# Hybrid decoder trunk: queries and keys as one product of 512 columns, pooling in alternating column halves, banks filled one by one, output weights prepared with a lead

## The chip, the cores and the metric

One core of a Trainium2 chip runs the whole program. The metric is the device time of one execution in microseconds. Three executions of the kernel before gave 939.35, 939.42 and 940.2 us; the median is 939.42. Profiles were taken of one execution each; there times are counted from the span's first instruction.

## The reference, cut to what matters

The trunk has two layers over 256 tokens of 1024 features. Each layer is a half-step feed-forward part, a mixer and another half-step feed-forward part, all in float32:

```
for l in range(DEPTH):                                  # DEPTH = 2
    x = x + 0.5 * swiglu(rms_norm(x, ffn1_norm[l]), ffn1_gate[l], ffn1_up[l], ffn1_down[l])
    h = rms_norm(x, mix_norm[l]) @ w_in[l]               # 1024 -> 18 blocks of 128
    y_pool = pool_mixer(u_pool, pool_w[l], pool_scale[l])
    y_moba = moba_attention(rope(qm), rope(km), vm)      # causal over 256 tokens, 4 heads of 64
    y_dil  = dilated_attention(rope(qd), rope(kd), vd)   # three dilations merged, 4 heads of 64
    y_conv = conv_module(u_conv, ...)                    # gate, 31 taps, layer norm, silu
    x = x + concatenate([y_pool, y_moba, y_dil, y_conv]) @ w_out[l]
    x = x + 0.5 * swiglu(rms_norm(x, ffn2_norm[l]), ffn2_gate[l], ffn2_up[l], ffn2_down[l])
return rms_norm(x, final_norm)
```

The inner width of the feed-forward parts is 2816, that is 22 blocks of 128. With 256 tokens, the whole attention of a head fits into 256 x 256 scores.

## The kernel before, in words

**Weights in two halves.** Every weight is used as a sum of two reduced-precision parts. Weights come in units of 128 x 2048 (a gate and an up block, half a down block, two blocks of the input projection or a quarter of the output projection). `prep` (L485) makes a unit ready in two halves: a load into one of four raw buffers (`RAW`), a ScalarE copy into the reduced type (`hi`), and a VectorE subtraction that gives the rest (`lo`). Five units can be ready at a time (`RING`, L41); a unit takes the place of the fifth one before it. The normed input is held the same way, `hi` and `lo` side by side. A product is then three terms, `hi` x `hi`, `hi` x `lo` and `lo` x `hi`.

**Gate, up and down.** `pair_unit` (L651) multiplies a gate and an up block with the input: 8 chunks of the contraction, two column blocks c with a PSUM bank each. `halves` (L624) issues for a list of (chunk, bank) items first all passes of one kind and then of the other: with `lo` weights a pass of 256 columns, with `hi` weights one of 512 (both parts of the input in one pass). The kind that comes first alternates from call to call. In `pair_units` (L639) the list runs over chunks, and inside over units and the two banks, so that the two banks take turns. The first unit behind a norm is issued in `BLOCKS` of chunks (0 to 3, 4 and 5, 6, 7), since the normed input comes chunk by chunk. At the start of the program three units are computed together, chunk by chunk, as their pieces arrive. Seven of the eight banks are given out by age (`oldest`).

**The mixer.** `mix` (L723) computes the convolution's gate and input with `pair_unit`, then, with tokens on the partitions, query and key of the dilated attention, values of both, query and key of the other attention, and the pooling input. `by_tokens` (L773) does one of them from one unit: 8 chunks x 2 token halves x 3 terms = 48 passes of 256 columns. `rope` (L786) calls it, copies the result out with a scale, rotates the first 16 features of each head by four small VectorE steps, transposes it back in four blocks and copies it out. The values (L840 to L853) are one product over two units with 512 columns per pass. `scores`, `softmax` and `pv` are the attention; `pv` issues its products for the two 64-column halves of the array in turn. Pooling (L885 to L907): after its input comes a product with a banded matrix for each of four groups (`psw`), a copy, a product with the group's weights (`psp`) and the copies out. The 31 taps of the convolution run on VectorE, the first four with help from ScalarE, then come bias, layer norm over the features (two rounds of small matmuls) and the last activation. The output projection (L943 to L952) takes four units in the order `W_OUT`: dilated attention, pooling, other attention, convolution; each is 48 passes of 256 columns.

**Order.** The program is first recorded as a list of operations with an estimated cost for each. `Plan.order` (L170) simulates the engines: each takes, of the operations that are ready, the one with the earliest due time, less a `lead` where one is set (L200 to L202); the order found is emitted, and on the chip every engine follows it strictly. `LEAD` (L51) is 0. The costs given to `mm`, `together` and `transpose` serve only this simulation.

**The end.** The last norm (L983 to L1015) needs its statistics, a transposed row of factors, and eight multiplications of 128 x 256 with stores: seven by VectorE out of PSUM, one by GpSimd from a copy that ScalarE made, whose store ScalarE issues. The program begins with ten warm-up matmuls (`WARM`, L46).

Of the kernel before, what the change touches and what calls it, by code (L numbers as in the profile page):

```python
# [16 lines left out]
T = 256  # L17
# [28 lines left out]
WARM = 10  # L46
# [4 lines left out]
LEAD = 0  # L51
# [19 lines left out]
class View:  # L71
# [23 lines left out]

    def heads(self):
        return self._then(lambda t: t.to_broadcast([128, 2, 4, t.shape[3]]))
# [166 lines left out]
def trunk(ctx: ExitStack, tc: tile.TileContext, d):  # L264
# [154 lines left out]
    units = []  # L419
    for l in range(DEPTH):  # L420
        for w in range(2):
# [63 lines left out]
    def prep():  # L485
# [5 lines left out]
        plan.lead = LEAD  # L491
# [76 lines left out]
    class Norm:  # L568
# [35 lines left out]
        def row(self, after):  # L604

            plan.hold = after
            for t in range(2):
                transpose(0.11, self.ps.on(t)[:, t * 128:(t + 1) * 128], self.col[:, t:t + 1].to_broadcast([128, 128]))
# [30 lines left out]
    def pair_units(nrm, names, blocks=ALL):  # L639
# [83 lines left out]
    def mix(l, nrm, after):  # L723
# [49 lines left out]
        def by_tokens(nm):  # L773
# [12 lines left out]
        def rope(i, j, nm, col):  # L786

            ps = by_tokens(nm)
            q = slot(i, f"{nm}t{l}")
            for t in range(2):  # L790
                A(T, q.on(t)[:, t], ps.on(t)[:, t], AF.Copy, scale=col[:, t:t + 1])
            v = q.rearrange("p t (h e) -> p t h e", h=4)
            a = work("ra", 2, [128, 2, 4, 16], f"ra_{nm}{l}")
            b = work("rb", 2, [128, 2, 4, 16], f"rb_{nm}{l}")
            tt(64, "tensor_mul", b.on(0)[:, :, :, 0:8], v[:, :, :, 8:16], sin_t[:, :, :, 0:8].heads())
            tt(64, "tensor_mul", b.on(1)[:, :, :, 8:16], v[:, :, :, 0:8], sin_t[:, :, :, 8:16].heads())
            tt(128, "tensor_mul", a, v[:, :, :, 0:16], cos_t.heads())
            tt(128, "tensor_add", v[:, :, :, 0:16], a, b)
            ps = bank("qk", 2, [128, 2, T], f"tr_{nm}{l}")
            for t in range(2):  # L800
                for c in range(2):
                    transpose(0.11, ps.on(2 * t + c)[:, c, t * 128:(t + 1) * 128], q[:, t, c * 128:(c + 1) * 128])
# [301 lines left out]
```

## Time and profile before

| what | us |
|---|---|
| median of three executions (939.35 to 940.2) | 939.42 |
| the profiled execution | 939.52 |
| its span, first to last instruction | 937.7 |
| TensorE matmul busy | 925.4 |
| VectorE busy | 717.7 |
| ScalarE busy | 561.7 |
| GpSimd busy | 33.6 |
| gate and up matmuls, share of the chain that ended last | 50% |
| down matmuls, share of that chain | 26% |

Busy time counts an engine as busy from the start to the end of an instruction. TensorE's matmuls overlap each other, so what one costs in a stream is read from the starts of two groups and not from its own duration. A stretch's wait is found in the idle time in brackets at the end of a timeline's row, with the engine that ended it. PE is TensorE, PEld its weight loads, DVE VectorE, ACT ScalarE.

### The profile page before, as it was taken

Reading aid. Unit: us, or ns where it says so; the run is one execution under the profiler, and the core shown is the slowest. Engines: PE = TensorE matmul, PEld = TensorE weight load, DVE = VectorE, ACT = ScalarE, POOL = GpSimd, SP = SyncE. Lnnn points to the kernel's source line nnn. Section 1 sums busy time; section 2 is a strip of 40 time slices with the busy share of each in tenths; the row PEclk is TensorE's granted clock in tenths of the full one; section 3 lists DMA queues with packets and bytes.
Section 4 is the critical chain, followed back from the end, with each engine's and each line's share of the span. In section 5 each row is a group of like instructions: output and inputs, shape, how many; then the busy total and the mean of one; then the engine's idle time right before and its main releaser. Section 6 shows DMA issues by size and latency. Waiting matters only on the chain.

```text
span 937.7 us, 15041 instructions
## 1 busy us (share of the span) xinstructions
PE 925.4 (99%) x5646; PEld 823.1 (88%) x5646; DVE 717.7 (77%) x1328; ACT 561.7 (60%) x1050; POOL 33.6 (4%) x46
## 2 busy tenths in 40 slices
PE   9999999999999999999999999999999999999996
PEld 8888888898898888888888888888988988888885
DVE  7789986679879988766778886668788989886652
ACT  7666664559576765554556565445667757555540
POOL 0000000100002000000100000011000200000010
PEclk9999999999999999999999999999999999999998
DMA  8855666762075765456755555567513476654641
GB/s 297 270 212 187 188 175 203 235 216 101 10 239 181 246 210 193 125 168 190 253 203 186 183 191 138 164 195 250 184 46 113 159 251 222 209 173 137 187 124 45
DMA packets 55209, 170.17 MB, mean 181 GB/s; under 512 B 6368, under 2 KB 8416, under 8 KB 55136
## 3 DMA queue, kind: packets, MB, share of 16 engines
q1 hardware_dynamic: 54560, 168.79, 55.7%
q8 instruction: 44, 0.72, 0.3%
q10 hardware_dynamic: 576, 0.42, 0.2%
q14 instruction: 29, 0.24, 0.1%
HBM read 168.14 MB, written 1.05 MB: 180 GB/s over the span
## 4 chain that ended last, share of the span: by engine, by line
PE 92%; DMA 3%; ACT 2%; DVE 2%; SPq 0%; issue 0%; ACTq 0%; DVEq 0%
PE mm_gu L368 50%; PE dn L368 26%; DMA raw<-in_gu_dram 3%; PE v L368 2%; PE wo L368 2%; PE pu L368 1%; PE qd L368 1%; PE qm L368 1%; PE kd L368 1%; PE km L368 1%; PE mm_cg L368 1%; PE mm_ca L368 1%; DVE y_f L346 1%; ACT hi L312 1%; DMA x<-in_x_dram 0%; DVE x L312 0%
## 5 line engine op out<-in xcount | busy, mean ns | idle before, releaser
L312 DVE TENSOR_TENSOR lo<-raw,hi 128x1024 fp32r<-128x1024 f32 (+3 forms) x365 | 386.3, 1085 | 68.1 <-ACT hi L312 54.4
L312 ACT ACTIVATE hi<-raw 128x1024 fp32r<-128x1024 f32 (+3 forms) x365 | 328.5, 940 | 136.1 <-PE dn L368 53.7
L368 PE MATMUL mm_gu<-y_f,hi 128*128 128x512 f32 x1408 | 332.4, 391 | 1.1 <-DVE t L312 0.8
L368 PEld LDWEIGHTS mm_gu<-y_f,hi 128*128 128x128 f32 x1408 | 260.6, 189 | 54.9 <-DVE y_f L346 1.9
L368 PEld LDWEIGHTS mm_gu<-y_f,lo 128*128 128x128 f32 x1408 | 176.1, 191 | 4.1
L368 PE MATMUL mm_gu<-y_f,lo 128*128 128x256 f32 x1408 | 178.3, 283 | 0.0
L368 PE MATMUL dn<-h,hi 128*128 128x512 f32 x704 | 169.4, 390 | 0.0
L368 PEld LDWEIGHTS dn<-h,hi 128*128 128x128 f32 x704 | 128.7, 188 | 24.1
L312 DVE TENSOR_TENSOR t<-mm_gu,t 128x256 f32<-128x256 f32 x176 | 66.9, 418 | 52.1 <-ACT t L312 51.7
L368 PEld LDWEIGHTS dn<-h,lo 128*128 128x128 f32 x704 | 91.5, 191 | 4.3
L368 PE MATMUL dn<-h,lo 128*128 128x256 f32 x704 | 92.8, 282 | 0.0
L312 ACT ACTIVATE h<-th 128x256 fp32r<-128x256 f32 x88 | 36.5, 417 | 70.2 <-DVE th L312 70.2
L312 ACT ACTIVATE t<-mm_gu 128x256 f32<-128x256 f32 x176 | 56.8, 375 | 26.9 <-PE mm_gu L368 26.8
L312 ACT ACTIVATE th<-t 128x256 f32<-128x256 f32 x88 | 36.7, 417 | 41.1 <-DVE t L312 31.1
L312 DVE TENSOR_TENSOR t<-t,rb_f 128x512 f32<-128x512 f32 x88 | 60.1, 686 | 0.8
L346 DVE SCALAR_TENSOR_TENSOR x<-dn,x 128x256 f32<-128x256 f32 x64 | 27.0, 422 | 38.0 <-PE dn L368 37.4
L368 PE MATMUL wo<-mx,hi 128*128 128x256 f32 x256 | 48.4, 289 | 0.0
L346 DVE SCALAR_TENSOR_TENSOR yv<-hpad,par,yv 128x256 f32<-128x256 f32 x108 | 44.3, 478 | 0.0
L312 DVE TENSOR_TENSOR th<-th,t 128x256 f32<-128x256 f32 x88 | 36.9, 420 | 9.0 <-ACT th L312 8.6
L368 PEld LDWEIGHTS wo<-mx,hi 128*128 128x128 f32 x256 | 39.9, 191 | 0.2
L312 DVE TENSOR_TENSOR h<-th,h 128x256 fp32r<-128x256 f32 x88 | 36.3, 418 | 1.1 <-ACT h L312 1.1
L368 PE MATMUL wo<-mx,lo 128*128 128x256 f32 x128 | 36.4, 284 | 0.0
(211 smaller groups left out, 677.0 us busy)
## 6 DMA issues: line engine op xcount, KB each, us to landing
raw<-in_gu_dram SPq DMA_DIRECT2D x170, 512.0 KB, 4.4
raw<-in_dn_dram SPq DMA_DIRECT2D x64, 384.0 KB, 3.6
raw<-in_dn_dram SPq DMA_DIRECT2D x64, 320.0 KB, 2.9
raw<-in_wi_dram SPq DMA_DIRECT2D x36, 512.0 KB, 4.4
raw<-in_wo_dram SPq DMA_DIRECT2D x16, 512.0 KB, 4.1
raw<-in_gu_dram SPq DMA_DIRECT2D x9, 256.0 KB, 5.7
con<-in_con_dram SPq DMA_DIRECT2D x1, 932.0 KB, 8.2
x<-in_x_dram SPq DMA_DIRECT2D x3, 256.0 KB, 5.7
```

The costliest lines, as they stand in the source:

```text
L312: f(*[val(x) for x in a], **{n: val(x) for n, x in k.items()})
L346: nc.vector.scalar_tensor_tensor(out, in0=a, scalar=scalar, in1=b, op0=op0, op1=op1)
L368: nc.tensor.matmul(val(o), lhsT=val(lhsT), rhs=val(rhs), start=self.i == 0, stop=self.i == self.n - 1, skip_group_check=True)
```

## The change

Queries and keys of one attention are computed by one product over two units, in the form that the values had (`wide`); `by_tokens` remains for the pooling input. `rope` then works by token half: two copies out, four rotation steps over the eight heads of query and key, four transposes; two copies at the end. The weights are laid out accordingly. In `pair_units` the banks are the outermost loop of a list. Pooling alternates between the two 64-column halves with each product, in two groups. Preparing an output unit (its loads, copies and subtractions) has a lead of 6 us in the planner. There is one warm-up matmul fewer; some of the planner's costs are changed; and at the end VectorE does all eight multiplications in order and SyncE issues all stores.

```diff
-WARM = 10
+WARM = 9
-LEAD = 0
+LEAD = 6.0
...
-    units = []
+    units, output = [], set()
...
                 for k in range(4):
+                    output.add(len(units))
                     units.append((d["wo"][l, k], 16))
...
-        plan.lead = LEAD
+        plan.lead = LEAD if n in output else 0.0
...
-            transpose(0.11, ps.on(t)[:, t * 128:(t + 1) * 128], y[:, t:t + 1].to_broadcast([128, 128]))
+            transpose(0.09, ps.on(t)[:, t * 128:(t + 1) * 128], y[:, t:t + 1].to_broadcast([128, 128]))
...
             i = halves([(s[u][c], ps[u][c], parts[u](2 * k + c), nrm.y[k])
-                        for k in range(a, b) for u in range(len(names)) for c in range(2)])
+                        for c in range(2) for k in range(a, b) for u in range(len(names))])
...
-                    s.mm(0.326, ps.on(t)[:, t], (xh, w[0]), (xh, w[1]), (xl, w[0]))
+                    s.mm(0.36, ps.on(t)[:, t], (xh, w[0]), (xh, w[1]), (xl, w[0]))
...
+        def wide(nm):
+
+            ps = [bank("mm", 4, [128, 512], f"{nm}{l}{t}") for t in range(2)]
+            sm = [Sum(), Sum()]
+            for u in range(2):
+                part = take()
+                for t in range(2):
+                    sl = slice(t * 128, (t + 1) * 128)
+                    for i in range(4):
+                        y = nrm.y[u * 4 + i]
+                        wh, wl = part(4 * i, 4)
+                        xh, xl = y.on(0)[:, 0, sl], y.on(1)[:, 1, sl]
+                        sm[t].mm(0.68, ps[t], (xh, wh), (xh, wl), (xl, wh))
+            return ps
+
+        def rope(i, j, nm):
+
+            ps = wide(f"qk{nm}")
+            out = [bank("qk", 2, [128, 2, T], f"tr_{n}{nm}{l}") for n in "qk"]
             for t in range(2):
+                qk = flat(slot(i + t, f"qk{nm}t{l}{t}"))
+                for n, col in enumerate((qcol, nrm.col)):
+                    s = slice(n * T, (n + 1) * T)
+                    A(T, qk.on(n)[:, s], ps[t][:, s], AF.Copy, scale=col[:, t:t + 1])
...
+                for n in range(2):
+                    for c in range(2):
+                        f = n * T + c * 128
+                        transpose(0.09, out[n].on(2 * t + c)[:, c, t * 128:(t + 1) * 128], qk[:, f:f + 128])
+            res = []
+            for n in range(2):
+                res.append(slot(j + n, f"{'qk'[n]}{nm}{l}"))
+                A(512, res[n], out[n], AF.Copy)
+            return res
...
-        qd = rope(8, 14, "qd", qcol)
-        kd = rope(9, 15, "kd", nrm.col)
+        qd, kd = rope(8, 14, "d")
...
-            together(1.8, *items)
+            together(1.45, *items)
...
-        qm = rope(8, 23, "qm", qcol)
-        km = rope(9, 24, "km", nrm.col)
+        qm, km = rope(8, 23, "m")
...
-        sw = [Sum(), Sum()]
-        for g in range(4):
-            c, e = g // 2, g % 2
-            o = psw.on(g)[64 * e:64 * e + 64, c]
-            ch = slice(64 * g, 64 * g + 64)
-            a = C_PW + g * PWN
-            sw[e].mm(0.14, o[:, 0:144], (ut.on(0)[:, 0, ch], con[:, a:a + 144]))
-            sw[e].mm(0.13, o[:, 128:256], (ut.on(1)[:, 1, ch], con[:, a + 144:a + 272]))
+        for c in range(2):
+            sw = [Sum(), Sum()]
+            o = [psw.on(c)[64 * e:64 * e + 64, c] for e in range(2)]
+            ch = [slice(64 * g, 64 * g + 64) for g in (2 * c, 2 * c + 1)]
+            a = [C_PW + g * PWN for g in (2 * c, 2 * c + 1)]
+            together(0.5, *[(sw[e], o[e][:, 0:144], ut.on(0)[:, 0, ch[e]], con[:, a[e]:a[e] + 144]) for e in range(2)],
+                     *[(sw[e], o[e][:, 128:256], ut.on(1)[:, 1, ch[e]], con[:, a[e] + 144:a[e] + 272])
+                       for e in range(2)])
...
-    row = work("sq", 2, [128, T], "row_fin")
-    A(T, row, ps[:, 0:T], AF.Copy)
-    for j in (6, 0, 1, 2, 3, 4, 5, 7):
+    for j in range(KC):
         o = scaled[j // 2].on(j % 2)[:, j % 2]
-        if j == 6:
-            gg(T, "tensor_mul", o, o, row)
-        else:
-            tt(T, "tensor_mul", o, o, ps[:, 0:T])
-        if j in (0, 1, 7):
+        tt(T, "tensor_mul", o, o, ps[:, 0:T])
+        if j in (0, 1, KC - 2, KC - 1):
             store(d["out"][:, j:j + 1], scaled[j // 2].on(j % 2)[:, j % 2:j % 2 + 1], 256)
-        elif j == 6:
-            rec("act", 0.47, nc.scalar.dma_start, [], [o], (), {
-                "out": d["out"][:, j:j + 1], "in_": scaled[j // 2].on(0)[:, 0:1]})
```

## Rows read from the trace of the kernel before

**Rows 1.** The page's first part: busy time, share of the span, instructions.
```profile
PE 925.4 (99%) x5646; PEld 823.1 (88%) x5646; DVE 717.7 (77%) x1328; ACT 561.7 (60%) x1050; POOL 33.6 (4%) x46
```

**Rows 2.** TensorE's waits, whole span: us in total, times, longest.
```profile
PE psp L368 <- ACT pl L312: 1.5, 2, 0.7
PE st_fin L312 <- DVE y_fin L346: 1.2, 1, 1.2
...
PE mm_gu L368 <- DVE t L312: 0.8, 1, 0.8
```

**Rows 3.** Windows: stretch, busy time (instructions) by engine, PEclk, DMA share, GB/s.
```profile
203.30:255.80 52.50, 51.76 (x393) 46.36 (x392) 45.23 (x137) 36.34 (x84) 0.00 (x0) 1.00 0.21 72
...
927.50:937.70 10.20, 1.39 (x11) 0.98 (x9) 3.97 (x14) 1.46 (x4) 0.72 (x1) 0.72 0.28 103
```

**Rows 4.** Timeline of TensorE, gate stage: start, us, instruction, tiles, shape, count.
```profile
28.03 4.00 PE L368 MATMUL mm_gu<-y_f,lo 128*128 128x256 f32 x32
31.86 7.44 PE L368 MATMUL mm_gu<-y_f,hi 128*128 128x512 f32 x32
39.14 4.00 PE L368 MATMUL mm_gu<-y_f,lo 128*128 128x256 f32 x32
```

**Rows 5.** Chain that ended last, first mixer: start, us on the chain, what.
```profile
218.96 2.06 PE v L368 x9
...
224.32 5.03 PE v L368 x21
229.34 5.75 PE qm L368 x48
...
237.62 0.44 PE tr_qm L312 x4
...
246.59 1.45 PE pv_d L380 x16
```

**Rows 6.** Timeline of TensorE, end of the first mixer's attention; idle before in brackets.
```profile
252.65 1.20 PE L368 MATMUL psw<-con,ut 128*64 128x144 f32 x16
254.59 1.13 PE L368 MATMUL psp<-pl,plw 128*128 128x256 f32 x4 [0.74 <-ACT pl L312]
...
255.99 0.39 PE L368 MATMUL wo<-mx,lo 128*128 128x256 f32 x1
...
263.62 0.70 PE L368 MATMUL ln<-yv,mean_w 128*128 128x256 f32 x2
```

**Rows 7.** Timeline of VectorE, same stretch and the seam behind it.
```profile
251.68 0.48 DVE L346 SCALAR_TENSOR_TENSOR yv<-hpad,par,yv 128x256 f32<-128x256 f32 x1
...
254.72 2.34 DVE L312 TENSOR_TENSOR lo<-raw,hi 128x1024 fp32r<-128x1024 f32 x2
...
275.15 0.75 DVE L346 SCALAR_TENSOR_TENSOR mx<-yv,mx 128x256 fp32r<-128x256 f32 x2
...
279.01 1.23 DVE L312 TENSOR_TENSOR lo<-raw,hi 128x1024 fp32r<-128x1024 f32 x1 [1.95 <-ACT hi L312]
```

**Rows 8.** Timeline of TensorE's weight loads at the start.
```profile
10.37 0.30 PEld L368 LDWEIGHTS mm_gu<-y_f,hi 128*128 128x128 f32 x2 [0.17 <-ACT hi L312]
...
11.59 0.30 PEld L368 LDWEIGHTS mm_gu<-y_f,hi 128*128 128x128 f32 x2 [0.34 <-ACT hi L312]
...
24.50 0.30 PEld L368 LDWEIGHTS mm_gu<-y_f,hi 128*128 128x128 f32 x2 [1.18 <-DVE t L312]
```

**Rows 9.** Timeline of TensorE, first unit of the second feed-forward part.
```profile
282.88 1.61 PE L368 MATMUL mm_gu<-y_f,hi 128*128 128x512 f32 x6
284.74 0.73 PE L368 MATMUL mm_gu<-y_f,hi 128*128 128x512 f32 x2 [0.25 <-DVE y_f L346]
```

**Rows 10.** Groups by shape, the warm-up: busy us, mean ns, idle before.
```profile
L368 PE MATMUL warm<-mean_w 128*128 128x128 f32 x20 | 4.6, 429 | 1.0 <-POOL half_pi L312 1.0
```

**Rows 11.** Timeline, all engines, the last norm.
```profile
931.33 0.38 ACT L312 ACTIVATE row_fin<-st_fin 128x256 f32<-128x256 f32 x1 [1.43 <-PE st_fin L312]
931.74 2.41 DVE L312 TENSOR_TENSOR xg<-xg,st_fin 128x256 f32<-128x256 f32 x7 [0.99 <-ACT row_fin L312]
```

More of the change, by code (lines that the diff above doesn't have):

```diff
@@ L782, in by_tokens @@
                     xh, xl = nrm.y[k].on(0)[:, 0, sl], nrm.y[k].on(1)[:, 1, sl]
-                    s.mm(0.326, ps.on(t)[:, t], (xh, w[0]), (xh, w[1]), (xl, w[0]))
+                    s.mm(0.36, ps.on(t)[:, t], (xh, w[0]), (xh, w[1]), (xl, w[0]))
             return ps
-        def rope(i, j, nm, col):
-            ps = by_tokens(nm)
-            q = slot(i, f"{nm}t{l}")
-            for t in range(2):
[L791 to L802, printed above, removed]
-            out = slot(j, f"{nm}{l}")
-            A(512, out, ps, AF.Copy)
-            return out
@@ new lines, in rope @@
+        def rope(i, j, nm):
+            ps = wide(f"qk{nm}")
+            out = [bank("qk", 2, [128, 2, T], f"tr_{n}{nm}{l}") for n in "qk"]
+            for t in range(2):
+                qk = flat(slot(i + t, f"qk{nm}t{l}{t}"))
+                for n, col in enumerate((qcol, nrm.col)):
+                    s = slice(n * T, (n + 1) * T)
+                    A(T, qk.on(n)[:, s], ps[t][:, s], AF.Copy, scale=col[:, t:t + 1])
+                v = qk.rearrange("p (h e) -> p h e", h=8)
+                a = work("ra", 2, [128, 8, 16], f"ra_{nm}{l}{t}")
+                b = work("rb", 2, [128, 8, 16], f"rb_{nm}{l}{t}")
+                sin, cos = sin_t[:, t], cos_t[:, t]
+                tt(64, "tensor_mul", b.on(0)[:, :, 0:8], v[:, :, 8:16], sin[:, :, 0:8].to_broadcast([128, 8, 8]))
+                tt(64, "tensor_mul", b.on(1)[:, :, 8:16], v[:, :, 0:8], sin[:, :, 8:16].to_broadcast([128, 8, 8]))
+                tt(128, "tensor_mul", a, v[:, :, 0:16], cos.to_broadcast([128, 8, 16]))
+                tt(128, "tensor_add", v[:, :, 0:16], a, b)
+                for n in range(2):
[7 more added lines that the diff above has]
+            return res
@@ L833, in softmax @@
             return p
-        qd = rope(8, 14, "qd", qcol)
-        kd = rope(9, 15, "kd", nrm.col)
+        qd, kd = rope(8, 14, "d")
         pd = [p for c in range(2) for p in scores(qd, kd, c, C_BD, f"d{l}", 16)]
-        psv = [bank("mm", 4, [128, 512], f"v{l}{t}") for t in range(2)]
+        psv = wide("v")
         vt = [flat(slot(20 + t, f"vt{l}{t}")) for t in range(2)]
-        sv = [Sum(), Sum()]
-        for u in range(2):
-            part = take()
-            for t in range(2):
-                sl = slice(t * 128, (t + 1) * 128)
-                for i in range(4):
-                    k = u * 4 + i
-                    wh, wl = part(4 * i, 4)
-                    xh, xl = nrm.y[k].on(0)[:, 0, sl], nrm.y[k].on(1)[:, 1, sl]
-                    sv[t].mm(0.65, psv[t], (xh, wh), (xh, wl), (xl, wh))
         for t in range(2):
@@ L1061 @@
     plw = np.zeros((DEPTH, 128, 2, 128), f32)
-    cols = [16, 17, 14, 15, 8, 9, 10, 11, 2, 3, 4, 5, 0, 1]
+    cols = [16, 17, 14, 15, 0, 1]
     for l in range(DEPTH):
@@ L1068 @@
         win = I["w_in"][l].reshape(KC, 128, 18, 128)
-        wi[l, [0, 1, 2, 3, 6, 7, 8]] = (win[:, :, cols].reshape(KC, 128, 7, 2, 128).transpose(2, 1, 0, 3, 4)
-                                        .reshape(7, 128, UNIT))
-        wi[l, 4:6] = win[:, :, [6, 7, 12, 13]].reshape(2, 4, 128, 512).transpose(0, 2, 1, 3).reshape(2, 128, UNIT)
+        wi[l, [0, 1, 8]] = (win[:, :, cols].reshape(KC, 128, 3, 2, 128).transpose(2, 1, 0, 3, 4)
+                            .reshape(3, 128, UNIT))
+        for u, four in ((2, [8, 9, 10, 11]), (4, [6, 7, 12, 13]), (6, [2, 3, 4, 5])):
+            wi[l, u:u + 2] = win[:, :, four].reshape(2, 4, 128, 512).transpose(0, 2, 1, 3).reshape(2, 128, UNIT)
         wot = I["w_out"][l].reshape(KC, 128, KC, 128)
```

8 lines of the change are left out of this document (3 added, 5 removed).

## The prediction

> **What bounds the kernel now.** I read the page's busy times first: TensorE is busy 925.4 of 937.7 us [rows 1], so only two things can move the end: fewer or shorter matmuls, or the 12 us in which it idles. Next the waits of TensorE [rows 2]: 1.5 us before the pooling weights (twice 0.74), 1.2 us in the last norm, 0.8 us behind an eviction at the start; the reader is to see how little is left to fill. Then busy time by stretch [rows 3]: in the attention stage TensorE idles 0.74 of 52.5 us at a granted clock of 1.00, while VectorE still has 7 us free; in the last 10.2 us TensorE works 1.4, and that tail is a chain of small steps and stores. Last the timelines of TensorE and VectorE for the price of a pass and for who is late at each seam [rows 4 to 11]. A change pays here if it takes columns or fixed cost out of the TensorE stream, or closes one of those seams. The profiled execution took 939.52 us, 0.1 above the median of 939.42; the sum is made against the former.
>
> **Queries and keys in passes of 512.** Removed: four times (two layers, two attentions) 96 passes of 256 columns; added: four times 48 of 512. In the steady gate stage 32 passes of 256 take 31.86 - 28.03 = 3.83 us, 119.7 ns each, and 32 of 512 take 39.14 - 31.86 = 7.28 us, 227.5 ns [rows 4]; both exceed their columns by the same 13 ns or so, and that is what a joined pair saves. In the products themselves 48 query passes take 5.75 us, 119.8 ns [rows 5]. The value product already has the form of the new one: 9 undisturbed passes take 2.06 us, 229 ns, but 21 of them behind a switch to the score matmuls take 5.03 us, 239.5 ns [rows 5]. So one joined product costs 48 x 229 = 10.99 us against 96 x 119.8 = 11.50: 0.51 saved, 2.0 us in all. The bounds are 2.3 us (227.5 ns) and nothing (239.5 ns); I take 229, since the switch to score matmuls stays where it was. The copies, the rotation and the transposes keep their number and size (four copies of 256, eight small VectorE steps, eight transposes for each pair), grouped by token half instead of by query and key; a group of four transposes costs TensorE 0.44 us before and after [rows 5]. The second half's copies, rotation and transposes now come after the whole product, some 3 us; the value product, and in the second attention the pooling product, run meanwhile and hide it. Without that cover it would be 3 us per attention.
>
> The Trainium skill, page "TensorE: Matmul & The Clock Gate", section "Back-to-back issue gap", speaks against this part: by it a warm pass costs its columns at 2.4 GHz and 2.5 ns more. Then 192 joined pairs would save 192 x 2.5 ns, an estimate of 0.5 us instead of 2.0. The 119.7 ns rows do not agree with it, since by its rule a pass of 256 takes 109 ns.
>
> **Pooling in alternating column halves.** The eight products (16 instructions) take 1.20 us per layer [rows 6]. The probability-value product, which alternates already, takes 1.45 us for 1536 columns [rows 5]; scaled to the pooling's 1088 columns that is 1.03, 0.17 less. Twice: 0.3 us, between 0 and 0.5.
>
> **Output weights prepared ahead.** The preparation of the output weights (one load, one ScalarE copy, one VectorE subtraction for each half) gets 6 us of priority in the planner. In the kernel before, the first two subtractions run from 254.72 to 257.06 [rows 7] and the first matmul that needs one stands at 255.99 [rows 6]. So when TensorE runs dry before the pooling weights at 253.85, there is nothing to fill it with: 0.74 us idle [rows 6]. With the subtractions earlier, output matmuls, whose other operand is ready by then, fill that hole; a switch back costs some 0.1. I take 0.6 per layer, 1.2 in all, between 0 and 1.5. What it passes: on SyncE's queue the loads of the next stage's weights wait behind the output weights' loads; on ScalarE and VectorE convolution taps and softmax steps wait, up to four subtractions of 1.2 us. Who waits for those: the convolution's normalisation, whose last tap ends at 252.16 [rows 7], but whose second averaging matmul comes only at 263.62 [rows 6]: some 9 us of room.
>
> **Banks one by one.** Both orders issue the same passes, so the rate stays. Three seams change. At the start the fourth unit has a free bank for its first column half but must wait for an eviction for the second; alternating, it stops after one pass, idle for 0.8 us on TensorE [rows 2] and 1.18 on its loads [rows 8]. One bank after the other, eight passes (1.8 us) stand before that wait and cover it. Against that, in the block paced by arriving weights the third unit's piece, ready at 11.59, is needed by the third pass and no longer by the fifth [rows 8]: two more passes of 227 ns lie behind it, 0.45 us later. Net -0.3, between -0.75 and +0.45. At the seam from the mixer to the second feed-forward the first block needs chunks 0 to 3 of the normed input after three passes, not six: where TensorE now runs six passes and waits 0.25 us till 284.74 [rows 9], it would have five and not two left behind that point, +0.7, and some 0.2 in the other layer. But that chain is late because a VectorE subtraction for a feed-forward weight, held up 1.95 us by its copy, stands in front of the residual sums from 279.01 to 280.24 [rows 7]; earlier output preparation frees the raw buffers that its load waits for. So between -0.3 and +0.9; the two effects oppose each other, and I take 0. In the middle of a stage the half unit needed up to 0.9 us sooner is long there: no wait for a weight is among TensorE's [rows 2].
>
> **One warm-up matmul fewer.** Ten take 4.6 us [rows 10], so 0.46 us at the head; the weights' arrival at 10.37 to 11.59 [rows 8] sets the pace anyway: 0.
>
> **The tail.** A ScalarE copy of the row and a GpSimd multiplication go, as does ScalarE's store; VectorE does eight multiplications instead of seven and SyncE issues six stores instead of five. VectorE starts only when ScalarE's copy of the same bank ends, 931.74 against 931.33 [rows 11]: 0.4 sooner, and one multiplication of 2.41/7 = 0.34 later. So 0, within 0.3.
>
> **Planner's costs** (transposes, probability-value product, passes) only reorder; TensorE has hardly any waits between its seams [rows 2], so I give that 0, within 0.5.
>
> Sum: -2.0 - 0.3 - 1.2 - 0.3 = -3.8 us, 935.7; against the median 935.6.
>
> **The rivals.** First, nothing gained in the passes: the joined products run at 239.5 ns like the value product's mean, the hole before the pooling weights stays because its chain (pooling copy, ScalarE's softmax steps, copy out) is as long as before, and the start loses its 0.45: -0.3 and +0.45, about 939.5. For it speaks that a mean of the existing 512 product is that slow; against it, that its undisturbed runs are not. The page's 0.5 us would fall between: with the other terms kept, -0.5 - 1.8 = -2.3, 937.1. It costs a chance of 0.07, as the rows speak against it.
>
> Second, slower: the convolution becomes last. The four earlier subtractions (4.9 us) go in front of taps, and TensorE reaches the fourth output unit sooner by 1.0 + 0.2 + 0.6 = 1.8 us per layer. Now that unit starts at 282.88 - 48 x 0.12 = 277.1 [rows 9], and its operand is done at 275.9 [rows 7]: 1.2 us of room. If the chain slid by the full 4.9 us, TensorE would wait 4.9 + 1.8 - 1.2 = 5.5 us in each layer, +11 - 3.8: 946.6. It decides from the point where the second averaging starts later than 263; the 9 us in which that chain now lies idle speak against it.
>
> Third, the parts work but the seam into the second feed-forward takes +0.9 and the start +0.45: 939.5 - 3.5 + 1.4 = 937.4.
>
> **How the numbers follow.** Forecast with its own bounds (934 to 937.5): 0.65. First rival 0.15, the page's figure 0.07, third 0.06, second 0.07. All parts at their best give 2.3 + 0.5 + 1.5 + 0.75 + 0.3 + 0.3 = 5.65, 933.8; upwards the range takes in the third rival and most of the way to the first: 933.7 to 938.9. 0.2% is 1.9 us, about what a measurement of this kernel can tell from no change; below 937.5 lie the forecast, the page's figure and half the third: 0.72. Slower (above 941.3) is the second rival: 0.07. The rest, 0.21, is the same.
>
> **What would show it.** Joined product: 48 passes near 229 ns, 11 us per product. TensorE's wait before the pooling weights under 0.2 us, with output matmuls in its place, and the output subtractions before 252. The start's wait for an eviction gone, the third unit's weight wait followed by four passes. VectorE's last multiplications start right behind the transposes. Wrong if the joined passes take 235 ns or more, if the output preparation still ends after 255, or if waits appear before the fourth output unit or the first feed-forward block.

## The result, and the profile after

| | median us | lowest to highest | executions |
|---|---|---|---|
| before, beside it on the same chip | 939.38 | 938.57 to 940.2 | 4 |
| after | 944.63 | 943.28 to 945.7 | 4 |

The ratio is 1.0054 with an interval of 1.0041 to 1.0067: 5.2 us slower, where 3.8 us faster was forecast, and outside the range. The profiled execution took 945.15 us, its span 943.1.

TensorE's waits over the whole span, the answer to [rows 2]; line numbers are 3 lower than before:

```profile
PE pt_m L309 <- DVE yv L343: 2.4, 2, 1.2
PE psp L365 <- ACT pl L309: 1.7, 2, 0.8
PE wo L365 <- DVE lo L309: 1.6, 2, 0.8
PE ln L365 <- DVE lsq L309: 1.3, 1, 1.3
PE st_f L309 <- DVE y_f L343: 1.2, 1, 1.2
...
PE mm_gu L365 <- ACT hi L309: 0.8, 1, 0.8
```

The wait in front of psp, which was to vanish, is there twice and longer; behind it stand new ones on the softmax (pt_m), on the output weights (wo) and on the convolution's layer norm (ln). The profile puts the first of these down to a tap (yv), but pt_m reads the softmax p_m, which ScalarE finishes at 255.06, just before pt_m starts at 255.11. To see where the time went, I cut each trace at four kinds of TensorE event: the first product of queries and keys, the end of the pooling input's product pu, the end of the output product wo, the end of the span. Below, qk..pu is called the attention stage, ..wo the output stage, and where the mixer is said to begin the first of these events is meant. Length of each stretch in us (starts and ends of matmuls from the timelines; the rows below "after" are the experiments that follow):

```
                        start  qk..pu  ..wo     ffn    qk..pu  ..wo    rest    span
before                 203.35  48.09  31.60  380.17   48.07  31.59  194.83   937.7
after                  202.85  47.17  35.38  379.60   47.01  35.40  195.69   943.1
joined alone           202.91  47.02  35.87  380.95   46.86  34.32  196.57   944.5
all but joined         203.71  48.07  31.59  380.44   48.05  31.59  194.85   938.3
costs alone            202.84  47.04  31.55  380.79   47.00  31.55  195.53   936.3
joined d only          203.44  47.47  31.58  380.87   47.49  31.59  194.46   936.9
joined m only          203.13  47.46  31.50  380.71   47.45  31.50  194.35   936.1
half taps, order kept  203.17  47.14  34.06  379.68   47.17  34.71  194.77   940.7
half taps, new order   202.94  46.96  30.44  381.08   47.20  30.45  194.93   934.0
whole taps, that order 203.69  54.18  30.44  380.83   53.59  30.45  195.12   948.3
convolution input 1st  203.26  47.04  31.51  381.36   47.09  31.51  195.33   937.1
five taps, no lead     203.90  47.03  30.45  381.82   47.05  30.46  195.69   936.4
banks alone            203.19  48.09  31.59  380.29   48.07  31.56  197.01   939.8
```

After against before: -0.50, -0.92, +3.78, -0.57, -1.06, +3.81, +0.86, together +5.4. The two attention stages are 2.0 us shorter, as forecast; the output stages lose 7.6. A stretch also changes when the order moves a matmul across its border, so these lengths alone don't price the joined products. The row "costs alone" shows it: it has no joined product and an attention stage as short, because seven matmuls (six of the second attention's scores, one of the averaging) stand behind pu there, where they and output matmuls leave TensorE no wait in front of psp. In "convolution input 1st" the stage holds exactly the matmuls that it holds before, but for the joined passes, and is 1.05 and 0.98 us shorter: 2.0 us is what the joining is worth.

What TensorE does in layer 1's output stage after (the answer to [rows 6]), and its busy time there and in layer 2 (columns as in [rows 3]):

```profile
250.81 1.15 PE L377 MATMUL psw<-con,ut 128*64 128x144 f32 x16
252.79 1.13 PE L365 MATMUL psp<-pl,plw 128*128 128x256 f32 x4 [0.84 <-ACT pl L309]
255.11 0.55 PE L309 MATMUL pt_m<-ident,p_m 128*128 128x128 f32 x3 [1.18 <-DVE yv L343]
...
256.69 0.39 PE L365 MATMUL wo<-mx,lo 128*128 128x256 f32 x1 [0.80 <-DVE lo L309]
...
263.38 1.13 PE L365 MATMUL ln<-yv,mean_w 128*128 128x256 f32 x4
...
268.31 0.58 PE L365 MATMUL ln<-ones,lsq 128*128 128x1 f32 x4 [1.29 <-DVE lsq L309]
```

```profile
250.06:285.40 35.34, 31.23 (x259) 29.12 (x260) 28.80 (x65) 28.07 (x63) 1.56 (x3) 1.00 0.60 193
712.05:747.41 35.36, 32.54 (x260) 30.60 (x261) 28.55 (x64) 27.95 (x63) 1.40 (x2) 0.95 0.58 191
```

In layer 1 TensorE idles 4.1 us here, in layer 2 2.8 us, and there its clock is down as well. The thing to see is the row at 263.38: the averaging of the convolution (ln), both halves of the features together. In the kernel before its first half stood at 251.28, right behind the last of pu, and the second at 263.62 [rows 6]:

```profile
251.28 0.59 PE L368 MATMUL ln<-yv,mean_w 128*128 128x256 f32 x2
```

And VectorE, the answer to [rows 7], with its first tap of the kernel before below it:

```profile
209.10 0.69 DVE L309 TENSOR_TENSOR ta<-ta,rb_m 128x512 f32<-128x512 f32 x1
209.91 2.36 DVE L309 TENSOR_TENSOR lo<-raw,hi 128x1024 fp32r<-128x1024 f32 x2
...
213.22 0.69 DVE L343 SCALAR_TENSOR_TENSOR hpad<-cth,ta 128x512 f32<-128x512 f32 x1
215.13 0.29 DVE L309 TENSOR_TENSOR ra_d<-qkdt,cos_t 128x128 f32<-128x128 f32 x1 [1.23 <-ACT qkdt L309]
...
219.45 0.43 DVE L309 CUSTOM_DVE_ANT_0 s_d<-qk_d,con 128x256 f32<-128x256 f32 x1 [2.03 <-PE qk_d L377]
...
223.84 0.46 DVE L343 SCALAR_TENSOR_TENSOR yv<-hpad,par,yv 128x256 f32<-128x256 f32 x1
...
254.65 0.86 DVE L343 SCALAR_TENSOR_TENSOR yv<-hpad,par,yv 128x256 f32<-128x256 f32 x2
255.42 1.22 DVE L309 TENSOR_TENSOR lo<-raw,hi 128x1024 fp32r<-128x1024 f32 x1
```

```profile
221.16 0.48 DVE L346 SCALAR_TENSOR_TENSOR yv<-hpad,par,yv 128x256 f32<-128x256 f32 x1
```

The taps begin at 223.84 (221.16 before) and end at 255.5 (252.16 before), although the mixer began 0.5 us earlier; up to the end of pu VectorE has done 49 of its 54 tap instructions, before 53. The five that are left (some 0.4 us each) stand between the softmax steps, and the output subtractions start behind them at 255.42, later than before (254.72 [rows 7]) in spite of their lead.

### The profile page after: what moved, and what is told of

The parts are those of the page before. It is cut to its first block, busy times and chain, and to the rows that moved or that the text cites. A ratio compares the mean times of both kernels' runs of the same rounds, so it can differ in the third digit from the quotient of the medians.

```text
span 943.1 us, 14685 instructions
## 1 busy us (share of the span) xinstructions
PE 924.2 (98%) x5452; PEld 813.8 (86%) x5452; DVE 722.1 (77%) x1329; ACT 564.9 (60%) x1049; POOL 32.5 (3%) x45
## 3 DMA queue, kind: packets, MB, share of 16 engines
HBM read 168.14 MB, written 1.05 MB: 179 GB/s over the span
## 4 chain that ended last, share of the span: by engine, by line
PE 91%; DVE 3%; DMA 3%; ACT 2%; issue 0%; DVEq 0%; SPq 0%; ACTq 0%
PE mm_gu L365 50%; PE dn L365 26%; PE v L365 2%; PE qkd L365 2%; PE qkm L365 2%; PE wo L365 2%; PE pu L365 1%; PE mm_cg L365 1%; PE mm_ca L365 1%; DMA raw<-in_gu_dram 1%; DVE lo L309 1%; DMA raw<-in_wo_dram 1%; ACT hi L309 1%; DVE y_f L343 1%; ACT s_m L309 1%; DMA x<-in_x_dram 1%
## 5 line engine op out<-in xcount | busy, mean ns | idle before, releaser
L309 DVE TENSOR_TENSOR t<-mm_gu,t 128x256 f32<-128x256 f32 x176 | 73.1, 421 | 42.8 <-ACT t L309 39.6
L309 ACT ACTIVATE t<-mm_gu 128x256 f32<-128x256 f32 x176 | 64.3, 374 | 30.0 <-PE mm_gu L365 30.0
```

Of the source, the lines that this page charges most:

```text
L309: f(*[val(x) for x in a], **{n: val(x) for n, x in k.items()})
```

## The experiments

**Which part of the change loses the time.** The first theory: the joined product delivers query and key together and late, the in-order queues of ScalarE and VectorE wait for it, and the taps slip. Rivals: the planner's changed costs, or one of the small parts. Four kernels:

```diff
 # joined alone: the kernel before with
+        qd, kd = rope(8, 14, "d")
+        qm, km = rope(8, 23, "m")
...
```

> The kernel before with the joined query-key product alone (its layout, its form of rotation; costs, lead, bank order, pooling, warm-up and end as before). Theory A, that the joined product delays the convolution's taps on ScalarE and VectorE and so the softmax and the output weights: at least 3 us slower than before, 942.5 or more, with TensorE idle 2.5 us or more in each output stage, although its 48 passes take 11 us per product. Rival B, that the planner's new costs and the lead spoil the order: 2 us faster, 937.5. Rival C, that the bank order does it: also 937.5.

946.5 us, ratio 1.0064 [1.0044, 1.0084].

```diff
 # all but joined: the kernel after with
-        qd, kd = rope(8, 14, "d")
+        qd = rope(8, 14, "qd", qcol)
+        kd = rope(9, 15, "kd", nrm.col)
...
```

> The changed kernel with queries and keys as four products of 256 columns again, all else as changed. Theory A: most of the loss is gone, 940.5 or less, last tap before 253.5 in the first layer. Rival B (costs and lead): it stays at 943 or more. Rival C (bank order): stays at 943 or more.

939.18 us, ratio 0.9993 [0.9984, 1.0003]. (The planner's costs of rope's transposes and of the value passes are those of the kernel before in it.)

```diff
 # costs alone: the kernel before with
-            transpose(0.11, ...)
+            transpose(0.09, ...)
-                    s.mm(0.326, ...)
+                    s.mm(0.36, ...)
-                    sv[t].mm(0.65, ...)
+                    sv[t].mm(0.68, ...)
-            together(1.8, *items)
+            together(1.45, *items)
```

> The kernel before with the planner's new costs alone (transposes 0.09, passes 0.36 and 0.68, probability-value product 1.45). Theory A: within 1 us of before. Rival B: 2 us slower or more. Rival C: within 1 us.

938.36 us, ratio 0.9984 [0.9975, 0.9993].

```diff
 # five taps, no lead: the kernel after with
-ATAPS = 4
+ATAPS = 5
-LEAD = 6.0
+LEAD = 0.0
```

> The changed kernel with the first five taps of the convolution prepared by ScalarE instead of four (VectorE then adds a 512-column product for two passes of 256 with a scalar) and no lead for the output weights. Theory A: VectorE's chain of taps gets shorter by some 0.2 us and the order is planned anew around it; if the late taps are the cause, TensorE's idle time in the output stages falls below 1.5 us each and the time to 939 or less. Rivals B and C: no change, 943 to 945.

936.54 us, ratio 0.9965 [0.9952, 0.9978]: faster than both kernels. So the joined products alone carry the whole loss, and they stop losing when one more tap is ScalarE's. In the table, the first and the last of these four differ in the output stages by 5.4 and 3.9 us.

**Lead or taps.** That kernel had two edits. One of them alone, and the other alone:

```diff
 # the kernel after with
-LEAD = 6.0
+LEAD = 0.0
```

> The kernel after, with the six-microsecond lead of the output weights' splitting set back to zero; everything else of the change stays. The run with five taps had two edits, five taps and no lead; this takes one of them alone. Theory A (the joined product holds ScalarE and VectorE up, the taps end too late, and the lead has little part in it): 943 to 946, VectorE's last tap still ends near 255 us and the waits of TensorE in the output stages stay over 5 us in all. Rival (the lead is at fault: subtractions put in front of taps): 940.5 or less.

948.85 us, ratio 1.0106 [1.0089, 1.0123]: slower still, more than either expectation.

```diff
 # the kernel after with
-ATAPS = 4
+ATAPS = 5
```

> The kernel after with one number changed: five taps by ScalarE in place of four (the lead of six microseconds stays). With the runs without the lead it closes a square of lead and taps: four taps 944.6 with and 948.9 without, five taps 936.5 without. If taps alone decide (theory A2), 935.5 to 938.5, and the averaging stands ahead of the output product again. If the lead's subtractions take the room on VectorE that five taps free: 939 or more, with waits of TensorE on lo or mx in the output stage.

937.59 us, ratio 0.9982 [0.9972, 0.9991]. The square is 944.6 and 937.6 with the lead, 948.9 and 936.5 without: the fifth tap brings 7 and 12 us, the lead helps only where the taps are late.

**What the joined passes are worth where they cost nothing.**

```diff
 # the kernel with five taps and no lead, with
-        qd, kd = rope(8, 14, "d")
+        qd = rope(8, 14, "qd", qcol)
+        kd = rope(9, 15, "kd", nrm.col)
...
```

> The kernel with five taps by ScalarE and no lead (936.5), but with queries and keys as four separate products of 256 features, as in the kernel before. Theory A (the joined passes are worth their 2 us where VectorE has room for the wait behind them): 938 to 939.3. Rival E (the five taps alone brought the gain, and the joined passes bring nothing on the path): 936 to 937.

938.26 us, ratio 0.999 [0.998, 0.9999], against 936.54 and 0.9965 with the joined ones: 1.7 us by the medians, 2.3 by the ratios, around the 2.0 of the forecast. Here too the two planner's costs named above go back with the products, so this is not the joining alone.

**Is VectorE late, or is it the written order?** The taps were cut to half their columns, first with every engine's order as it was, then with an order made anew for the shorter taps:

```diff
 # order kept
-    stt(T, o, src(c, k), wcol(c, k), o, ALU.mult, ALU.add)
+    stt(T, o[:, 0:128], src(c, k)[:, 0:128], wcol(c, k), o[:, 0:128], ALU.mult, ALU.add)
```

> The kernel after with its order of instructions untouched on every engine, but each of VectorE's 54 taps per layer worked on 128 of its 256 columns (so the convolution lacks 27 of its 31 taps in half of the tokens). VectorE is given back some 7 us per layer ahead of the softmax and the layer norm, and nothing else moves. Theory A (what is late in the output stage is VectorE, behind taps that began late): the waits of TensorE on p_m, yv, lo, lsq and y_f in the output stages (together 8 to 9 us) shrink to under 2 and the time comes to 937 to 939. Rival D (the order itself: ScalarE's in-order places, the transfers of the raw weights, or the gaps of TensorE that bring its clock down): 942.5 or more.

943.12 us, ratio 1.0044 [1.0029, 1.0059]: VectorE's relief, some 7 us per layer, brings 1.5, and the interval overlaps that of the kernel after. The same edit in the kernel before:

> The same halving of VectorE's taps in the kernel before (27 of 31 taps lack half of the tokens), its order untouched. Theory A says that the taps were covered there: only the 0.74 us in front of psp in each layer, which are ScalarE's, stand in its output stages, so 938.4 to 939.4. If the taps had bound the stage already before: 937 or less, and then the halving in the kernel after says less.

939.36 us, ratio 1.0003 [0.9994, 1.0013]: in the kernel before, the taps were covered. And the kernel after once more, with the planner told of the shorter taps:

```diff
-    stt(T, o, src(c, k), wcol(c, k), o, ALU.mult, ALU.add)
+    stt(128, o[:, 0:128], src(c, k)[:, 0:128], wcol(c, k), o[:, 0:128], ALU.mult, ALU.add)
```

> The kernel after, with the same half-width taps as in the run before (27 of 31 taps lack half of the tokens), but the order is now worked out anew with the shorter duration: the convolution's averaging then stands some 12 us earlier in TensorE's queue, between the pooling and the output product. VectorE's work is that of the other half-tap run; only the order differs. Theory A2 (what costs is the order that is written out around late taps: TensorE's queue has nothing between the pooling and the softmax): 936.5 to 939, and from the end of pu to the end of wo 30.5 to 31.6 us in each layer in place of 34.1 to 35.4. Rival D (transfers of the raw weights, or ScalarE's own load): 942 or more, with 34 us there again.

936.55 us, ratio 0.9965 [0.9951, 0.9979]. The same instructions in another order are 6.6 us faster. TensorE in that kernel, the end of the attention, and its output stage:

```profile
249.74 0.59 PE L365 MATMUL ln<-yv,mean_w 128*128 128x256 f32 x2
250.26 0.93 PE L377 MATMUL qk_m<-km,qm 64*128 64x128 f32 x8
251.12 1.15 PE L377 MATMUL psw<-con,ut 128*64 128x144 f32 x16
252.19 0.70 PE L365 MATMUL ln<-yv,mean_w 128*128 128x256 f32 x2
253.80 1.02 PE L365 MATMUL psp<-pl,plw 128*128 128x256 f32 x4
```

```profile
249.90:280.34 30.44, 30.44 (x259) 28.72 (x258) 21.42 (x53) 25.16 (x58) 0.74 (x1) 1.00 0.51 174
```

The averaging and pieces of wo now fill the time in which pooling's copy and the softmax run; nothing is idle. When TensorE's queue holds the averaging behind the output product, finishing the taps sooner gives TensorE nothing to do. The next run takes this order (its planner is told 128 columns), but whole taps:

```diff
-    stt(T, o, src(c, k), wcol(c, k), o, ALU.mult, ALU.add)
+    stt(128, o, src(c, k), wcol(c, k), o, ALU.mult, ALU.add)
```

> The kernel after, complete, with all its instructions at full width, but written out in the order that was worked out for taps of half the duration (the planner is told the shorter duration, the taps themselves are whole). Theory A2 in its strict form (the written order alone costs; VectorE could do the whole taps in time): 936.5 to 939, no wait of TensorE on yv or ln over 0.5 us, and 30.4 to 31 us from the end of pu to the end of wo. Rival N (the order only mirrors taps that are truly late, so forcing it moves the wait to the averaging): 940 or more, with TensorE waiting for yv in front of ln near 250 us, 2 us or more in each layer, and psw, psp and wo queued behind it.

950.2 us, ratio 1.0119 [1.0099, 1.0138]. The strict form of the theory falls: the wait moves. Its one new wait of TensorE, and VectorE's row that holds it up:

```profile
PE tr_qm L309 <- DVE qkmt L309: 10.0, 2, 5.0
```

```profile
234.42 9.59 DVE L343 SCALAR_TENSOR_TENSOR yv<-hpad,par,yv 128x256 f32<-128x256 f32 x24
```

The second rotation (qkmt) stands behind 24 taps, and TensorE waits 5 us per layer for it. (It was expected in front of ln.) The two attention stages are 7.2 and 6.4 us longer than in the run before, more than these waits: the granted clock was 0.50 from 242.7 to 249.5 and 0.51 from 710.3 to 713.8. So whole taps don't fit into that order. Whether they fit into another one, this run leaves open; the last run of the next part answers it.

**Both products or one.** 

```diff
 # joined d only: the kernel after with, for m, the product of the kernel before
-        qm, km = rope(8, 23, "m")
+        qm = rope1(8, 23, "qm", qcol)
+        km = rope1(9, 24, "km", nrm.col)
...
```

> The kernel after with the first pair of queries and keys (d) as one joined product and the second pair (m) as two of 256 features. Theory G (the loss comes from the first joined product, whose rotation makes VectorE wait 2 us for the scores and brings the four taps on ScalarE and with them VectorE's taps back by 2.7 us): 942 to 946, VectorE's taps begin near 223.8 us. Theory H (neither alone: only both together push the convolution's averaging behind the output product): 937.5 to 940.5.

938.52 us, ratio 0.9985 [0.9976, 0.9994].

```diff
 # joined m only
-        qd, kd = rope(8, 14, "d")
+        qd = rope1(8, 14, "qd", qcol)
+        kd = rope1(9, 15, "kd", nrm.col)
...
```

> The kernel after with the second pair of queries and keys (m) as one joined product and the first pair (d) as two of 256 features. Theory G: VectorE's taps begin near 221 us as in the kernel before, and with one joined product's 1 us gained the time is 938 to 940. Theory H: 937.5 to 940.5 too, so the two are told apart by the run with d alone; if this one is slow instead (942 or more), the scores of m, which come late and together, are at fault and both theories fall.

938.08 us, ratio 0.9985 [0.9975, 0.9994]. Each alone is harmless and makes the attention stage 0.6 us shorter in each layer. That the first joined product as such delays the taps is thereby refuted: with d alone they begin at 218.6.

**Why VectorE is late only there.** In the kernel after, VectorE has 47.2 us for some 42.7 us of work in that stage (40.66 busy and five taps of 0.4 left over), yet it idles 6.5. In the rows above, ta is ready at 209.8, but the step that makes the convolution's input from it (hpad) stands behind two subtractions and the first rotation, at 213.22. ScalarE, which makes the products of the first four taps from it, waits for the second half of the joined product meanwhile:

```profile
214.26 0.47 ACT L309 ACTIVATE qkdt<-qkd,qc 128x256 f32<-128x256 f32 x1 [1.88 <-PE qkd L365]
...
214.99 0.90 ACT L309 ACTIVATE yv<-hpad,par 128x256 f32<-128x256 f32 x2
```

So both engines wait while taps could run if hpad stood earlier. The next run moves that step:

```diff
+        plan.lead = 6.0
         stt(512, hpad.on("h")[:, :, PADC:], th, 1.0, ta, ALU.add, ALU.mult)
+        plan.lead = 0.0
```

> The kernel after, complete, with one operation of 0.7 us per layer given a lead of six microseconds: the last step of the convolution's input (hpad). In the kernel after VectorE does it at 213.22 us, behind two subtractions and the first rotation, though its operands are ready at 209.8; in the fast kernels with one joined product or with five taps it is done at 210.4 to 210.9, ScalarE makes its taps while TensorE is still in the joined product, and VectorE's taps begin at 218.5 in place of 223.8. Theory P (that step's place in VectorE's queue decides whether the joined product's waits are filled with taps): 937 to 940.5, hpad at 210.5 to 211, VectorE's taps from 219 to 221, 54 of 54 taps done before the pooling, and the averaging back ahead of the pooling's second product. Rival Q (the place of that step is a symptom; VectorE lacks the time in any case): 943 or more, or the waits return in front of tr_qm or ln.

938.28 us, ratio 0.9984 [0.9975, 0.9994]: 6.3 us back from the place of one step of 0.68 us and what the order makes of it. VectorE there, and the end of TensorE's attention:

```profile
211.47 0.68 DVE L343 SCALAR_TENSOR_TENSOR hpad<-cth,ta 128x512 f32<-128x512 f32 x1
...
216.36 1.48 DVE L309 TENSOR_TENSOR yv<-yv,gt 128x512 f32<-128x512 f32 x2
217.88 1.28 DVE L343 SCALAR_TENSOR_TENSOR yv<-hpad,par,yv 128x256 f32<-128x256 f32 x3
...
248.07 0.47 DVE L343 SCALAR_TENSOR_TENSOR yv<-hpad,par,yv 128x256 f32<-128x256 f32 x1
```

```profile
250.14 0.59 PE L365 MATMUL ln<-yv,mean_w 128*128 128x256 f32 x2
...
252.60 0.70 PE L365 MATMUL ln<-yv,mean_w 128*128 128x256 f32 x2
253.46 1.13 PE L365 MATMUL psp<-pl,plw 128*128 128x256 f32 x4 [0.16 <-ACT pl L309]
```

hpad runs 1.75 us earlier (half a us later than expected), the taps begin 6 us earlier (at 217.9, a us before the expectation), all 54 are done at 248.5, and the averaging is back ahead of psp. So VectorE has the time for whole taps, and rival Q falls. Its idle time in the first layer's attention stage goes with the result: 6.5 us in the kernel after and 7.2 with the joined products alone, against 4.4 here, 3.4 with five taps and no lead and 2.6 with d alone (and 6.0 in the kernel before, whose stage is 0.9 us longer). Nor is the loss a chance of a single order: with both products joined, four taps by ScalarE and hpad unmoved, four different orders took 944.1 to 948.9 us. What remains unseparated is the step's own place from the rest of the order that the planner made with it. Its place isn't the only way in: in the kernel with m alone hpad stands at 213.49, and the taps, with room behind separate products, still begin at 220.6.

**Banks one by one, and the lead, alone.**

```diff
 # banks alone: the kernel before with
-                        for k in range(a, b) for u in range(len(names)) for c in range(2)])
+                        for c in range(2) for k in range(a, b) for u in range(len(names))])
```

> The kernel before with only the order of the gate products changed: all blocks of one bank, then the next. The prediction put its gain at 0.3 us at the start, within -0.75 to +0.45, and nothing elsewhere: 939.1. The trace of after has 0.5 us less up to the first mixer, which fits. Rival (that 0.5 us came from the planner's changed durations, since the runs with the durations changed but banks as before reach the mixer as early): 939.4 to 940, and the mixer's first product starts at 203.3 us as before.

941.75 us, ratio 1.0026 [1.0015, 1.0038]: slower, by 2.2 us in the last stretch of the table. The row of each engine in the second layer's last feed-forward part:

```profile
758.01 1.06 ACT L312 ACTIVATE hi<-raw 128x1024 fp32r<-128x1024 f32 x1 [1.10 <-DMA raw<-in_gu_dram]
```

```profile
759.10 1.23 DVE L312 TENSOR_TENSOR lo<-raw,hi 128x1024 fp32r<-128x1024 f32 x1 [0.88 <-ACT hi L312]
760.25 0.15 DVE L353 TENSOR_SCALAR v_f<-st_f 128x2 f32<-128x2 f32 x1
```

```profile
762.42 0.43 PE L312 MATMUL st_f<-ident,y_f 128*128 128x128 f32 x2 [1.53 <-DVE y_f L346]
```

A raw weight lands late, its copy and subtraction follow, and the subtraction stands on VectorE in front of the eleven small steps of the norm's factor, and TensorE waits 1.5 us for that factor (in the kernel before that subtraction ends at 758.08 and nothing waits). The kernel after has the same picture at 765.8, 1.2 us. But undoing the banks there,

```diff
-                        for c in range(2) for k in range(a, b) for u in range(len(names))])
+                        for k in range(a, b) for u in range(len(names)) for c in range(2)])
```

> The kernel after with the gate products' banks mixed as in the kernel before; the rest of the change stays. Theory K (banks one by one cost about 2 us wherever they are, because a subtraction of a gate weight whose raw data lands late is queued on VectorE in front of the 2 us chain of y_f; the kernel after shows the same wait, 1.2 us at 765.8): 942 to 943.5, and no wait for y_f over 0.6 us in the second layer's last FFN. Rival L (in the kernel after, where that FFN begins 4.5 us later, the wait comes from elsewhere): 944.3 or more.

gave 944.11 us, ratio 1.0058 [1.004, 1.0077], no different from after and between the two expectations. In its trace the wait for y_f in that part is gone and the last stretch 1.2 us shorter, as theory K has it, but the start, with the wait for an eviction back (0.9 us), is 1.2 longer and the feed-forward stretch 1.1. And the same edit in the kernel with five taps and no lead

> The fastest kernel so far (five taps by ScalarE, no lead, 936.5) with the gate products' banks mixed as before. Theory K: 933.5 to 936, since the waits for y_f in front of mm_gu and st_f (3.2 us in all there) shrink. Rival L: 936.3 to 937.5, the banks being worth nothing or a little gain once the order fits.

gave 935.52 us, ratio 0.9956 [0.9939, 0.9973], the lowest median of all, though its interval overlaps that of 936.54. The 2 us don't add up across kernels; the traces point to which subtraction the order puts there, but no run moves that alone. Last, the lead:

```diff
 # the kernel before with
-LEAD = 0
+LEAD = 6.0                  # for the output units alone
```

> The kernel before with the lead of six microseconds for the output weights' splitting alone. The prediction gave it 1.2 us (it fills the 0.74 us in front of psp in both layers): 937.9 to 938.4. Rival M (the lead moves transfers and subtractions, but not the work that TensorE lacks between the pooling and the softmax, so the wait for pl stays at 1.5 us): 939 to 940; if it brings the subtractions in front of the taps, 940.5 or more.

940.15 us, ratio 1.0008 [0.9999, 1.0018], and psp waits 1.5 us as before.

## Why the prediction was wrong

**Joined passes: right in size, wrong in cover.** The stream's gain was forecast at 2.0 us and is 0.92 + 1.06 in the attention stages; the second joined product takes 10.88 us, 226.7 ns a pass, the first 2.84 + 8.18 = 11.02 (both from the chain). The Trainium skill, page "TensorE: Matmul & The Clock Gate", section "Back-to-back issue gap", has for an isolated warm matmul a gap that makes an estimate of 215.8 ns at 512 columns (512/2.4 + 2.5) and of 0.5 us for the saving; for a stream of weight loads and matmuls of 512 it gives about 131 ns. The measured 226.7 ns and 2.0 us agree with neither and decide here. The step that failed is the sentence that the value and pooling products hide the second half's copies, rotation and transposes. They hide them for TensorE, which has no wait there, but the forecast put what follows at nothing: the output stages, for which -1.5 us was forecast (lead and pooling), took 7.6 us more. I never asked what the waiting costs the waiting engines. VectorE was read as having 7 us free [rows 3]; those were waits in an in-order queue. With the joined product there are waits of 1.23, 0.70, 2.03 and 0.73 us around the first rotation; the stage's idle time grew from 6.0 to 6.5 us while the stage became 0.9 us shorter. What was left no longer held the taps, and their averaging was what TensorE did while pooling's copy and the softmax ran.

**Planner's costs "only reorder": forecast 0 within 0.5.** Alone they brought 1 to 1.5 us (0.9984 of before), in part by what the lead was to do: output matmuls and the averaging fill the time in front of psp, and TensorE has no wait in either output stage. In the larger sense the claim was the main error: the change alters the graph that the planner orders, and the order was worth 6 to 12 us between kernels whose work is nearly the same.

**Lead: forecast -1.2, measured nothing.** It gave the output weights priority, but the first subtraction came at 255.42, which is the prediction's own sign of being wrong, and psp still waits 0.84 us. In the fast kernels that hole is filled by the averaging, and in several by output matmuls too. Filling it is no gain by itself: with all but the joined products the output matmuls stand there as forecast and psp doesn't wait, but the next operand of wo isn't ready,

```profile
PE wo L368 <- DVE mx L312: 1.8, 2, 0.9
```

and the output stage takes 31.59 us as before. Why the kernel after without the lead is 4.2 us slower isn't settled: the table for it would show +0.9 at the start, +1.7 and +1.0 in the feed-forward parts and -0.6 in the output stages, that is mostly places where no output weight is prepared, which speaks for the order again; no run shows it.

**Pooling: forecast -0.3, measured nothing.** The products take 1.15 us in place of 1.20 [rows 6], but from their start to psp it is 1.98 against 1.94 us: the copy of the result ends it.

**Banks: forecast -0.3, measured some 2.4 us slower alone** (0.15% to 0.38%), outside its bounds. The start's gain of 0.5 us looked like a hit, but with the costs alone the mixer begins as early (202.84) and with the banks alone it hardly moves (203.19). The wait for an eviction went as forecast, and one of 0.8 us for a weight came. The loss sits in layer 2, in front of the transposes of the norm's factor, some 20 us behind the start of the seam that I had priced (0.7 in layer 1, 0.2 in the other); whose subtraction stands in front of that factor's chain I had not looked at.

**Tail and warm-up: right, 0.** VectorE's eight multiplications (2.74 us) start 0.46 us after the transposes' start, where it took 0.93 before [rows 11]; from there to the end of the span it is 6.79 against 6.89 us.

**The rivals.** The slower one (946.6, chance 0.07) had the sign, nearly the time, and the convolution, but not the mechanism: it wanted four earlier subtractions in front of the taps and a wait before the fourth output unit. The subtractions came later, and all waits but one stand ahead of the third of the 192 output passes in each layer; that one (1.29 us, layer 1) stands in the second unit. None of my cases had taps that slip because VectorE waits for the joined product, so the chance of slower was far too small. The chances also have a slip: forecast, the Trainium skill's figure and half the third make 0.65 + 0.07 + 0.03 = 0.75 below 937.5, not 0.72. And the best case leaves out the planner's 0.5.

## What to carry to other kernels

Free time of an in-order engine is only room for more delay if work that is ready stands in its queue where the delay falls; before a product is merged, list for each engine behind it what is queued after the wait, and who needs that next. Where a program orders the instructions, a change of the graph or of a cost is worth as much as the new order, here up to 12 us for one number; so price a change with its order's first consequences (which filler stands in TensorE's queue while the softmax runs), and try the neighbouring settings before judging it. Five taps by ScalarE beside the joined products are faster than either kernel.

## What the hardware showed that I had not expected

The same idle pattern cost clock in one layer and not in the other. Stretches of the kernel after, columns as in [rows 3]:

```profile
712.05:718.68 6.63, 3.81 (x33) 2.58 (x34) 4.86 (x22) 5.99 (x23) 0.00 (x0) 0.99 0.00 0
718.68:723.02 4.34, 4.34 (x24) 4.34 (x25) 4.26 (x7) 3.16 (x10) 0.00 (x0) 0.62 0.68 224
...
250.06:256.00 5.94, 3.81 (x33) 2.58 (x33) 4.17 (x20) 5.30 (x20) 0.00 (x0) 1.00 0.00 0
256.00:262.00 6.00, 5.31 (x45) 5.17 (x47) 4.95 (x8) 5.33 (x16) 0.00 (x0) 1.00 0.68 205
```

In both layers TensorE was busy 3.81 of some 6 us. In layer 2 the granted clock of the next 4.3 us was 0.62, so most of it at 1.2 GHz, and 19 output passes took 1.86 + 1.83 = 3.69 us (chain) where 0.12 each makes 2.28: 1.4 of that layer's 3.8 us. In layer 1 it stayed at 1.00. Other slow kernels scatter likewise: with the joined products alone the clock was 0.50 from 258.1 to 261.5 us, in layer 1 only; in the kernel after with the banks mixed it was 0.50 in both layers (257.9 to 261.3 and 722.1 to 725.5). The four executions of the kernel after have mean clocks of 0.993 to 0.995, so a part of the loss differs between executions of one kernel. No run here separates why.
